# An identity product for the old state, both solve copies on ScalarE, and one matrix that adds and centers the two directions in an RWKV-7 recurrence

## The chip, the cores and the metric

One NeuronCore of a Trainium2 chip runs the whole program: a trunk of four layers (gated spatial units, an RWKV-7 mixer, latent attention, gated spatial units again) on 256 context and 256 input positions of width 1024. The metric is the device time of one execution in microseconds (us). The engines are TensorE (PE; its weight loads are shown apart as PEld), VectorE (DVE), ScalarE (ACT), GpSimd (POOL) and SyncE (SP), which issues most of the transfers. PE writes only into PSUM, an accumulation memory of eight banks; DVE and ACT read it.

## The reference, cut to what matters

The change lies in the RWKV-7 mixer, the second layer. Its recurrence runs over the positions in both directions, the context first, and carries one 64x64 state per head and direction:

```
def step(S, inp):
    w_t, k_t, v_t, kk_t, a_t = inp[:5]
    s_kk = einsum('nbhvk,nbhk->nbhv', S, kk_t)
    S = S * w_t[..., None, :] - s_kk[..., :, None] * (kk_t * a_t)[..., None, :] \
        + v_t[..., :, None] * k_t[..., None, :]
    y_t = einsum('nbhvk,nbhk->nbhv', S, inp[5])
    return S, y_t
...
y = ys[0] + jnp.flip(ys[1], axis=1)          # forward + reversed backward

yh = split_heads(y)                          # group norm over each head's 64 values
mean = jnp.mean(yh, axis=-1, keepdims=True)
var = jnp.mean(jnp.square(yh - mean), axis=-1, keepdims=True)
yn = ((yh - mean) * lax.rsqrt(var + RWKV_LN_EPS)).reshape(y.shape) * ln_gain + ln_bias
```

## The kernel before, in words

The 16 heads are taken in four groups g = 0 to 3 of four heads. The 512 positions are cut into chunks of 64, so each group has eight chunk steps (i = 0 to 7), four for the context (c = 0) and four for the input (c = 1). A step treats four "lanes" l (two directions by two pairs of heads), each with two heads h, which lie in partitions 0 to 63 and 64 to 127.

Five flows, written as generators, are interleaved in the program text in fixed ratios:

- `features` (L639 to L704) makes the per-position factors of the next group: decay scans, exponentials and the operands `AR` and `BK`, on PE, ACT, DVE and POOL.
- `inverse` (L706 to L770) inverts the triangular matrices of the next group: 31 pairs of DVE instructions, `tmp` (L734) and `Tm` (L735), each needing the one before it, and then small products on PE.
- `operands` (L774 to L807) masks products (`pe` on PE, `E` on DVE, L789) and transposes (`pbk`, `BKT`) for the next two steps.
- `chain` (L809 to L876) is the recurrence, described below.
- `gate`, `normed` and `added` (L878 to L973): products `pg` for the gate, the group norm, and the output projection `op`, which is added to `xT`.

One step of `chain`: 16 products into `pz` (the last eight read the old state `s0`), copied to `Z` by ACT; eight products into `pu`, the solve, copied into `UV` in two halves, partitions 64 to 127 by ACT (L839) and partitions 0 to 63 by DVE (L840); eight products `py` of the old state (L845); eight products `pd` (L852), to which DVE adds the old state (L856) and which it then scales by the chunk's decay (L857) to give the new state `S`; eight more products into `py` (L861). Then `Y` takes the outputs of the step. The two directions reach a place of `Y` at different steps: whichever comes first is copied there by ACT (L870, steps with c < 2), the other is added by DVE (L872, steps with c >= 2), the backward one with its positions reversed.

`normed` multiplies `Y` by `bdm`, a block matrix of 1/64, into `pmean` (L937), subtracts that from `Y` on DVE (L938), squares on ACT (L941), multiplies by `bdm` again into `pvar` (L943), takes Ln and Exp on ACT (L278, L279), and multiplies `Y` by the result on DVE (L945).

PSUM in this part: one bank each for the tags f, n and t, two for s, three for c. All of `pz`, `pu`, `py`, `pd` and `pg`, and for g < 3 `pmean`, `pvar`, `bon` and `op`, take turns in the three banks of c. The order on each engine is not the order of the text: a scheduler places the instructions when the program is built, with its own estimate of durations, and gives out the buffers as it goes; each engine then runs its own list in that order.

Of the kernel before, what the change touches and what calls it, by code (L numbers as in the profile page):

```python
# [8 lines left out]
F32 = mybir.dt.float32  # L9
F32R = mybir.dt.float32r  # L10
AF = mybir.ActivationFunctionType
ALU = mybir.AluOpType
# [86 lines left out]
def body(tc, I, out):  # L99
    nc = tc.nc  # L100
# [347 lines left out]
    def rwkv(m):  # L448
# [3 lines left out]
        bdm = const.tile([128, 128], F32, name="bdm")  # L452
        V.tensor_scalar(bdm, bd, 1.0 / 64, None, ALU.mult)
        half = const.tile([128, 5, 8], F32, name="half")
        V.tensor_scalar(half[:, 0:4, :], vec[:, 6:10, :], 0.5, None, ALU.mult)
# [353 lines left out]
        def chain(g, f):  # L809
# [4 lines left out]
            for i in range(8):  # L814
# [24 lines left out]
                S.copy(uv[H[1], 0, ii], pu[H[1]])  # L839
                V.tensor_copy(uv[H[0], 1, ii], pu[H[0]])  # L840

# [7 lines left out]
                if i < 7:  # L849
                    pd = q4(ps("pd", "c"))  # L850
                    for l, h in LH:
                        PE.matmul(pd[H[h], l], bk[:, l, h, :], uv[:, h, ii, l], start=True, stop=True)  # L852
                    sn = ct("S", [128, 4, 64], 2)
                    pcb = f["12"][:, :, i:i + 1].to_broadcast([128, 4, 64])
                    if s0 is not None:
                        V.tensor_tensor(sn, pd, s0, ALU.add)  # L856
                        V.tensor_tensor(sn, sn, pcb, ALU.mult)  # L857
                    else:
                        V.tensor_tensor(sn, pd, pcb, ALU.mult)
                for l, h in LH:  # L860
# [5 lines left out]
                c, yt = i % 4, f["Y"][i // 4]  # L866
                for n in range(2):
                    y = yt[:, :, (3 - c) * 64:(4 - c) * 64][:, :, ::-1] if n else yt[:, :, c * 64:c * 64 + 64]
                    if c < 2:
                        S.copy(y, py[:, n * 2:n * 2 + 2])  # L870
                    else:
                        V.tensor_tensor(y, y, py[:, n * 2:n * 2 + 2], ALU.add)  # L872
                if i < 7:
# [54 lines left out]
        def normed(g, f, c, b=None, q=ALL):  # L928

            if b is None:  # L930
                b = ct("fin", [128, 2, 256], 3)
                yield from bonus(g, c, b)
            cut, flat = quarters(q)
            tags = iter("fn" if g == 3 else "cc")
            y, z, b = cut(f["Y"][c]), cut(f["z"][c]), cut(b)
            pm = flat(ps("pmean", next(tags)))
            PE.matmul(pm, bdm, y, start=True, stop=True)  # L937
            V.tensor_tensor(y, y, pm, ALU.subtract)  # L938
            yield
            sq = cut(ct("fin", [128, 2, 256], 3))  # L940
            S.activation(sq, y, AF.Square)  # L941
            pq = flat(ps("pvar", next(tags)))
            PE.matmul(pq, bdm, sq, start=True, stop=True)  # L943
            state["act"] = rsqrt_bc(sq, pq, 1.0, epsln)
            V.tensor_tensor(y, y, sq, ALU.mult)  # L945
            yield
            for pr in range(2):
                o = g * 2 + pr
                V.scalar_tensor_tensor(out=y[:, pr], in0=y[:, pr], scalar=hvec[:, 1, o:o + 1], in1=b[:, pr], op0=ALU.mult, op1=ALU.add)
            state["dve"] = V.tensor_tensor(y, y, z, ALU.mult)  # L950
            yield
# [5 lines left out]
        def added(g, f, c, tags, q=ALL, ws=None):  # L957

            cut, flat = quarters(q)
            y = cut(f["Y"][c])  # L960
            for oo in range(4):
# [70 lines left out]
        for g in range(4):  # L1032
# [5 lines left out]
            for c in range(2):  # L1038
                f["Y"].append(ct("Y", [128, 2, 256], 3))
                if (g, c) == (3, 1):  # L1040
# [355 lines left out]
```

## Time and profile before

| | us |
|---|---|
| three runs: lowest, median, highest | 1627.23, 1627.66, 1628.16 |
| the profiled execution, its own time | 1626.01 |
| its span, first to last instruction | 1623.8 |
| PE busy (matmuls), weight loads | 1521.5 (94%), 1182.9 (73%) |
| DVE, ACT, POOL busy | 1173.6 (72%), 786.9 (48%), 123.3 (8%) |
| the recurrence, from the first `pz` to the last output product | about 665 to 1053 |

The span is 2.2 us shorter than the profiled execution's own time. Busy shares are of the whole span. PE's busy time is modelled from pipelined starts, so a full PE row need not be PE at its peak. Of the 388 us of the recurrence three stretches of some 41 us (699.68 to 740.52, 801.94 to 843.40 and 910.51 to 951.50) hold the DVE part of the `inverse` of groups 1, 2 and 3, and the 66 us from 972 to 1038 hold the chain of group 3, which has no next group to prepare.

### The profile page before, as it was taken

The numbers are of one execution on the slowest core, as the hardware profiler recorded it, in microseconds if no ns is written. First come the engines' busy times: TensorE is split into PE (matmuls) and PEld (weight loads), VectorE is DVE, ScalarE is ACT, GpSimd is POOL, SyncE is SP. The second block draws the span as 40 slices with busy tenths as digits, with TensorE's granted clock in tenths as the row PEclk, the third lists the DMA queues.
The fourth block names the chain that finished last, engine by engine and source line by source line (L and its number), as shares of the span: only waits on it lengthen the run. The fifth ranks groups of instructions, "written<-read, shape, count | busy, mean of one in ns | idle before, by whom it ended". The sixth has DMA issues, their size and how long they took to land.

```text
span 1623.8 us, 28689 instructions
## 1 busy us (share of the span) xinstructions
PE 1521.5 (94%) x11538; PEld 1182.9 (73%) x11538; DVE 1173.6 (72%) x2133; ACT 786.9 (48%) x1404; POOL 123.3 (8%) x156
## 2 busy tenths in 40 slices
PE   5999999999599998999999999889999999979999
PEld 2787888888466644776776777778777777768887
DVE  3789998844878376687877964778765666665876
ACT  4534321232456343435345333469876766456543
POOL 0000000000600232302203100000000000000000
PEclk9999999999799998899999999989999999989999
DMA  9675668531144552522322132144321232265552
GB/s 363 252 281 226 233 212 306 208 104 52 52 143 169 161 164 66 157 92 76 118 91 85 61 106 88 67 144 136 118 83 43 73 99 91 66 233 186 177 182 78
DMA packets 95173, 229.03 MB, mean 141 GB/s; under 512 B 26048, under 2 KB 52160, under 8 KB 80576
## 3 DMA queue, kind: packets, MB, share of 16 engines
q1 hardware_dynamic: 92736, 223.00, 40.6%
q10 hardware_dynamic: 2304, 4.20, 0.7%
q8 instruction: 91, 1.49, 0.4%
q14 instruction: 42, 0.34, 0.1%
HBM read 208.81 MB, written 17.83 MB: 140 GB/s over the span
## 4 chain that ended last, share of the span: by engine, by line
PE 49%; DVE 14%; ACT 3%; issue 2%; POOL 1%; DMA 1%; ACTq 0%; DVEq 0%
PE fm L310 5%; PE op L310 4%; PE op L966 2%; PE fm L311 2%; PE pg L895 2%; DVE Tm L735 2%; DVE tmp L734 2%; PE op L311 2%; PE pu L310 2%; PE pz L310 2%; PE po L1277 2%; PE sc L1295 2%; PE pe L785 2%; PE sc L1296 1%; DVE BK L695 1%
## 5 line engine op out<-in xcount | busy, mean ns | idle before, releaser
L184 DVE TENSOR_TENSOR lo<-raw,hi 128x2048 fp32r<-128x2048 f32 (+3 forms) x147 | 247.1, 1682 | 105.2 <-ACT hi L183 104.5
L183 ACT CAST hi<-raw 128x2048 fp32r<-128x2048 f32 (+3 forms) x161 | 212.3, 1324 | 217.5 <-PE op L314 40.5
L251 DVE SCALAR_TENSOR_TENSOR junk<-adaw,scb 128x1024 f32<-128x1024 f32 x112 | 136.8, 1222 | 8.7 <-DMA adaw<-in_ada_wT 6.7
L310 PE MATMUL op<-s,hi 128*128 128x512 f32 x256 | 91.5, 400 | 0.0
L375 PE MATMUL pv<-hi,hp 128*128 128x512 f32 x192 | 76.4, 400 | 9.1 <-ACT hi L183 6.0
L376 PE MATMUL pv<-lo,hp 128*128 128x512 f32 x192 | 76.2, 397 | 1.7 <-DVE lo L184 1.7
L310 PE MATMUL fm<-hx,hi 128*128 128x512 f32 x200 | 73.8, 409 | 4.1 <-ACT hx L304 3.8
L377 PE MATMUL pv<-hi,hp 128*128 128x512 f32 x192 | 75.9, 395 | 0.0
L311 PE MATMUL op<-s,lo 128*128 128x256 f32 x256 | 71.3, 281 | 0.0
L895 PE MATMUL pg<-xz,wz 128*128 128x256 f32 x256 | 68.7, 408 | 0.0
L313 PE MATMUL pj<-xs,hi 128*128 128x512 f32 x128 | 53.6, 420 | 12.5 <-ACT xs L304 10.2
L311 PE MATMUL fm<-hx,lo 128*128 128x256 f32 x200 | 56.6, 288 | 2.0 <-DVE lo L184 2.0
L995 PE MATMUL pv<-wv,xv 128*128 128x512 f32 x128 | 57.3, 596 | 0.0
L310 PEld LDWEIGHTS op<-s,hi 128*128 128x128 f32 x256 | 48.0, 188 | 12.4 <-issue 1.3
L314 PE MATMUL pj<-xs,hi 128*128 128x512 f32 x128 | 52.2, 408 | 5.0 <-DVE xs L305 5.0
L694 POOL TENSOR_TENSOR BK<-f 64x256 f32<-64x256 f32 x64 | 53.5, 836 | 38.1 <-DVE f L688 30.7
L785 PE MATMUL pe<-AR,BK 64*128 64x128 f32 x512 | 53.8, 306 | 2.2 <-DVE E L789 2.0
L310 PE MATMUL fm<-cq,hi 128*128 128x512 f32 x144 | 55.7, 423 | 0.0
L895 PEld LDWEIGHTS pg<-xz,wz 128*128 128x128 f32 x256 | 47.8, 198 | 10.0 <-issue 2.1
L315 PE MATMUL pj<-xs,lo 128*128 128x512 f32 x128 | 52.1, 408 | 2.2 <-DVE lo L184 2.1
L313 PE MATMUL pu<-hp,hi 128*128 128x512 f32 x128 | 50.7, 396 | 0.0
L789 DVE TENSOR_TENSOR E<-pe,masks 128x512 f32<-128x512 f32 x64 | 41.9, 683 | 12.1 <-PE pe L785 7.2
(392 smaller groups left out, 4063.2 us busy)
## 6 DMA issues: line engine op xcount, KB each, us to landing
adaw<-in_ada_wT SPq DMA_DIRECT2D x36, 1024.0 KB, 6.2
raw<-in_sgu_v SPq DMA_DIRECT2D x16, 1024.0 KB, 5.5
raw<-in_sgu_u SPq DMA_DIRECT2D x16, 1024.0 KB, 4.9
raw<-in_sgu_z SPq DMA_DIRECT2D x16, 1024.0 KB, 4.8
raw<-in_sgu_o SPq DMA_DIRECT2D x16, 1024.0 KB, 4.8
adaw<-in_ada_w SPq DMA_DIRECT2D x24, 512.0 KB, 10.0
xz<-xz SPq DMA_DIRECT2D x32, 256.0 KB, 3.0
raw<-in_ml_z SPq DMA_DIRECT2D x16, 512.0 KB, 3.7
```

The lines of the kernel that those rows point to most:

```text
L183: S.copy(hi[:, sl], raw[:, sl])
L184: (nc.gpsimd if parts > 1 and i else V).tensor_tensor(lo[:, sl], raw[:, sl], hi[:, sl], ALU.subtract)
L251: V.scalar_tensor_tensor(out=junk, in0=raw[:, f, :], scalar=1.0, in1=scb[:, c, :], op0=ALU.mult, op1=ALU.mult, accum_out=m[:, t * 2 + f, c ...
L310: PE.matmul(p, whi, x, start=start, stop=False)
L311: PE.matmul(p[:, 0:256], wlo, x[:, 0], start=False, stop=stop)
L313: PE.matmul(p, whi, x[:, 0], start=start, stop=False)
L375: PE.matmul(pv[tb], hs[k][:, 0, sl], whi[:, ws_], start=k == 0, stop=False)
L376: PE.matmul(pv[tb], hs[k][:, 0, sl], wlo[:, ws_], start=False, stop=False)
L377: PE.matmul(pv[tb], hs[k][:, 1, sl], whi[:, ws_], start=False, stop=k == 7)
L785: PE.matmul(pe[h][:, j * 128:j * 128 + 128], bk[H[h], i % 4, :, :], ar[H[h], i % 4, :, :], start=True, stop=True)
L895: PE.matmul(p, ws[k // 4][:, k % 4, pr * 128:pr * 128 + 128], xs[k // 2][:, k % 2, :], start=k == 0, stop=k == 7)
L995: PE.matmul(p, xv[:, k, tb * 128:tb * 128 + 128], ws[k // 4][:, k % 4, :], start=k == 0, stop=k == 7)
```

## The change

Three edits in the recurrence and its norm, and a buffer for them.

1. The second half of the solve copy goes from DVE to ACT (L842 of the new file), behind the first.
2. In the 24 steps that have an old state and need a new one (six in each group), two products with the identity matrix put the old state into `pd` before its own products add to it: 128 partitions by 64 columns of `ident`, once for each half of the partitions, over all 256 columns of the state. DVE then only scales.
3. Both directions' outputs are copied by ACT, the forward ones to `Y`, the backward ones (reversed) to a second tile `Yr`. The norm multiplies both by `center`, the identity minus `bdm`, into one `pmean`. That is the centered sum, so the subtraction goes, and square and scaling read `pmean`, which now keeps its bank until the scaling.

```
+        center = const.tile([128, 128], F32, name="center")
+        V.tensor_tensor(center, ident, bdm, ALU.subtract)
...
                 S.copy(uv[H[1], 0, ii], pu[H[1]])
-                V.tensor_copy(uv[H[0], 1, ii], pu[H[0]])
+                S.copy(uv[H[0], 1, ii], pu[H[0]])
...
-                    pd = q4(ps("pd", "c"))
+                    pd = ps("pd", "c")[:, 0:256]
+                    if s0 is not None:
+
+                        for h in range(2):
+                            PE.matmul(pd[H[h]], ident[:, H[h]], s0.rearrange("p l v -> p (l v)"), start=True, stop=False, skip_group_check=True)
+                    pd = pd.rearrange("p (l v) -> p l v", l=4)
                     for l, h in LH:
-                        PE.matmul(pd[H[h], l], bk[:, l, h, :], uv[:, h, ii, l], start=True, stop=True)
+                        PE.matmul(pd[H[h], l], bk[:, l, h, :], uv[:, h, ii, l], start=s0 is None and l == 0, stop=l == 3, skip_group_check=True)
                     sn = ct("S", [128, 4, 64], 2)
-                    pcb = f["12"][:, :, i:i + 1].to_broadcast([128, 4, 64])
-                    if s0 is not None:
-                        V.tensor_tensor(sn, pd, s0, ALU.add)
-                        V.tensor_tensor(sn, sn, pcb, ALU.mult)
-                    else:
-                        V.tensor_tensor(sn, pd, pcb, ALU.mult)
+                    V.tensor_tensor(sn, pd, f["12"][:, :, i:i + 1].to_broadcast([128, 4, 64]), ALU.mult)
...
-                for n in range(2):
-                    y = yt[:, :, (3 - c) * 64:(4 - c) * 64][:, :, ::-1] if n else yt[:, :, c * 64:c * 64 + 64]
-                    if c < 2:
-                        S.copy(y, py[:, n * 2:n * 2 + 2])
-                    else:
-                        V.tensor_tensor(y, y, py[:, n * 2:n * 2 + 2], ALU.add)
+                S.copy(yt[0][:, :, c * 64:c * 64 + 64], py[:, 0:2])
+                S.copy(yt[1][:, :, (3 - c) * 64:(4 - c) * 64][:, :, ::-1], py[:, 2:4])
...
-            PE.matmul(pm, bdm, y, start=True, stop=True)
-            V.tensor_tensor(y, y, pm, ALU.subtract)
+            PE.matmul(pm, center, y, start=True, stop=False)
+            PE.matmul(pm, center, cut(f["Y"][c][1]), start=False, stop=True)
             yield
             sq = cut(ct("fin", [128, 2, 256], 3))
-            S.activation(sq, y, AF.Square)
+            S.activation(sq, pm, AF.Square)
             pq = flat(ps("pvar", next(tags)))
             PE.matmul(pq, bdm, sq, start=True, stop=True)
             state["act"] = rsqrt_bc(sq, pq, 1.0, epsln)
-            V.tensor_tensor(y, y, sq, ALU.mult)
+            V.tensor_tensor(y, pm, sq, ALU.mult)
...
-                f["Y"].append(ct("Y", [128, 2, 256], 3))
+                f["Y"].append([ct("Y", [128, 2, 256], 3), ct("Yr", [128, 2, 256], 3)])
...
-    nc = _bacc.Bacc("TRN2", target_bir_lowering=False, num_devices=1)
+    nc = _bacc.Bacc("TRN2", target_bir_lowering=False, num_devices=1, dynamic_dma_scratch_size=1024)
```

The scheduler places everything anew from the first step on. On PE, the step of group 0 around the first norm's `pvar` stood thus before (`wx` and `w2w`, `l2w` are operands of `features`; in brackets the engines that a row waits for):

```order
L845 MATMUL py<-AR_3905,S 64x64 x2
L845 MATMUL py<-AR_4057,S 64x64 x2
L643 MATMUL pw<-wx,w2w 128x512
L644 MATMUL pw<-wx,l2w 128x512
L852 MATMUL pd<-UV,BKT 64x64 [waits Activation_49]
L861 MATMUL py<-E,UV 64x64
L852 MATMUL pd<-UV,BKT 64x64 [waits DVE_49]
L852 MATMUL pd<-UV,BKT 64x64 x6
L861 MATMUL py<-E,UV 64x64 x7
L895 MATMUL pg<-xz,wz 128x256 [waits PE_49]
```

After the change the same step reads on PE:

```order
L645 MATMUL pw<-wx,w2w 128x512
L646 MATMUL pw<-wx,l2w 128x512
L847 MATMUL py<-AR_3849,S 64x64 [waits Activation_49]
L847 MATMUL py<-AR_3849,S 64x64
L847 MATMUL py<-AR_4001,S 64x64 x2
L847 MATMUL py<-AR_3907,S 64x64 x2
L847 MATMUL py<-AR_4059,S 64x64 x2
L863 MATMUL py<-E,UV 64x64 [waits Activation_49]
L856 MATMUL pd<-S,ident 64x256 [waits PE_49,Activation_49]
L856 MATMUL pd<-S,ident 64x256
L859 MATMUL pd<-UV,BKT 64x64 x8
L863 MATMUL py<-E,UV 64x64 x7
```

The identity products stand right before the other products of `pd` and wait for ACT; of the 24 pairs, 14 have that wait, five wait for DVE, four for PE alone and one for nothing. The old-state products of `py`, which waited for nothing from ACT, now do in this step.

On ACT, at the same place before (L278 and L279 are Ln and Exp of the norm):

```order
L833 COPY Z<-pz 128x256
L278 ACT_TABLE_LOAD
L278 ACTIVATE fin<-pvar,epsln 128x512
L839 COPY UV<-pu 64x256
L279 ACT_TABLE_LOAD
L279 ACTIVATE fin<-fin 128x512
L658 ACTIVATE f<-pw,half 128x512
```

And after:

```order
L835 COPY Z<-pz 128x256
L278 ACT_TABLE_LOAD
L278 ACTIVATE fin<-pvar,epsln 128x512
L841 COPY UV<-pu 64x256
L279 ACT_TABLE_LOAD
L279 ACTIVATE fin<-fin 128x512
L842 COPY UV<-pu 64x256
```

The second solve copy stands behind a table load and the Exp. It does so in five of the seven norms over whole tiles; in the other two it follows the first copy directly.

## Rows read from the trace of the kernel before

**Rows 1.** Windows by stretch: start:end, length, busy PE, PEld, DVE, ACT, POOL, clock, DMA.
```profile
699.68:740.52 40.84, 39.16 (x563) 30.72 (x560) 39.22 (x100) 13.61 (x28) 1.49 (x1) 1.00 0.30 92
801.94:843.40 41.46, 38.35 (x557) 30.18 (x557) 39.20 (x99) 12.83 (x27) 1.51 (x1) 1.00 0.32 104
910.51:951.50 40.99, 37.56 (x555) 29.80 (x555) 39.09 (x99) 12.26 (x26) 0.00 (x0) 1.00 0.31 93
972.00:1038.00 66.00, 64.20 (x896) 50.12 (x895) 29.26 (x67) 23.20 (x51) 0.00 (x0) 1.00 0.29 97
1038.00:1053.00 15.00, 12.39 (x88) 11.42 (x86) 14.51 (x51) 10.38 (x28) 0.00 (x0) 1.00 0.01 2
sum 388.00, PE 360.61 PEld 279.90 DVE 287.90 ACT 168.45 POOL 61.02; mean PE 40.07 PEld 31.10 DVE 31.99 ACT 18.72 POOL 6.78
```

**Rows 2.** The page's chain that ended last, whole span, shares by engine.
```profile
PE 49%; DVE 14%; ACT 3%; issue 2%; POOL 1%; DMA 1%; ACTq 0%; DVEq 0%
```

**Rows 3.** Groups by line: busy us, mean ns of one, idle before and releaser.
```profile
L840 DVE COPY UV<-pu 64x256 f32<-64x256 f32 x32 | 13.1, 410 | 22.0 <-ACT UV L839 22.0
L839 ACT COPY UV<-pu 64x256 f32<-64x256 f32 x32 | 11.7, 367 | 32.9 <-PE pu L838 29.3 <-DMA xz<-xz 3.2
L856 DVE TENSOR_TENSOR S<-pd,S 128x256 f32<-128x256 f32 x24 | 10.0, 418 | 4.9 <-PE pd L852 4.8
L872 DVE TENSOR_TENSOR Y<-Y,py 128x128 f32<-128x128 f32 x32 | 8.5, 282 | 0.0
L870 ACT COPY Y<-py 128x128 f32<-128x128 f32 x32 | 7.0, 271 | 11.0 <-PE py L861 11.0
```

**Rows 4.** Instructions of tile Y: ns least/median/most, first and last start.
```profile
L938 DVE TENSOR_TENSOR Y<-Y,pmean x9: 421/681/687, 712.5 to 1040.0; 128x512 f32<-128x512 f32 x7, 128x256 f32<-128x256 f32 x2
```

**Rows 5.** PE's order of time around a step: start, length, instruction, count of records.
```profile
668.62 0.69 PE L852 MATMUL pd<-UV,BKT 128*64 128x64 f32 x16
669.14 0.64 PE L861 MATMUL py<-E,UV 128*64 128x64 f32 x16
669.70 0.32 PE L829 MATMUL pz<-UV,E 64*64 64x64 f32 x2
```

**Rows 6.** The chain that ended last, in order of time: start, us, what.
```profile
972.03 1.92 PE pg L895 x8
975.04 1.05 PE pmean L937 x2
```

**Rows 7.** Windows of the state addition L856 on DVE, by stretch: length, busy, count.
```profile
699.68:740.52 40.84, 1.63 (x4) 1.00 0.30 92
801.94:843.40 41.46, 1.25 (x3) 1.00 0.32 104
910.51:951.50 40.99, 1.41 (x4) 1.00 0.31 93
972.00:1038.00 66.00, 2.53 (x6) 1.00 0.29 97
```

**Rows 8.** Windows of the subtraction L938 on DVE, the same.
```profile
699.68:740.52 40.84, 0.68 (x1) 1.00 0.30 92
972.00:1038.00 66.00, 1.79 (x3) 1.00 0.29 97
```

**Rows 9.** Sum of the windows of L840 over the three inverse stretches.
```profile
sum 123.29, DVE 4.49; mean DVE 1.50
```

**Rows 10.** Sum of the windows of L872 over the three inverse stretches.
```profile
sum 123.29, DVE 2.23; mean DVE 0.74
```

**Rows 11.** What PE waited for from 665 to 1053: us in total, times, longest.
```profile
PE pd L852 <- DVE UV L840: 6.8, 6, 2.2
PE pd L852 <- ACT UV L839: 1.8, 5, 0.6
```

**Rows 12.** ACT's order of time at the first norm.
```profile
717.85 0.37 ACT L839 COPY UV<-pu 64x256 f32<-64x256 f32 x1
718.24 1.28 ACT L279 ACT_TABLE_LOAD   x1
719.53 0.63 ACT L279 ACTIVATE fin<-fin 128x512 f32<-128x512 f32 x1
```

More of the change, by code (lines that the diff above doesn't have):

```diff
@@ L934, in normed @@
             tags = iter("fn" if g == 3 else "cc")
-            y, z, b = cut(f["Y"][c]), cut(f["z"][c]), cut(b)
+            y, z, b = cut(f["Y"][c][0]), cut(f["z"][c]), cut(b)
             pm = flat(ps("pmean", next(tags)))
-            PE.matmul(pm, bdm, y, start=True, stop=True)
-            V.tensor_tensor(y, y, pm, ALU.subtract)
+            PE.matmul(pm, center, y, start=True, stop=False)
+            PE.matmul(pm, center, cut(f["Y"][c][1]), start=False, stop=True)
             yield
             sq = cut(ct("fin", [128, 2, 256], 3))
-            S.activation(sq, y, AF.Square)
+            S.activation(sq, pm, AF.Square)
             pq = flat(ps("pvar", next(tags)))
@@ L959, in added @@
             cut, flat = quarters(q)
-            y = cut(f["Y"][c])
+            y = cut(f["Y"][c][0])
             for oo in range(4):
```

## Prediction

> **What bounds the kernel now.** I read the page's chain of waits first, then windows cut where the work changes character, then the waits on PE. Over the whole span the chain that ended last runs half on PE, 49%, and 14% on DVE [rows 2]. The change touches only the recurrence, 665 to 1053 us, so that is where its worth has to be read. There PE is busy 360.6 of 388 us and DVE 287.9 [rows 1]. The reader is to see two regimes in the stretches. In the three that hold the DVE part of the inverse, 123.3 us together, both engines are nearly full: DVE 117.5 us, PE 115.1 us, so PE idles 8.2 us. In the last group, 972 to 1038, PE is busy 64.2 of 66 us and DVE only 29.3. The remaining 183.7 us (the total less these and the 15 us tail) hold 169.0 us of PE. So PE is the engine that has least room everywhere, and DVE is its equal in the inverse stretches only. The change takes work from DVE and gives some to ACT and some to PE.
>
> **What is removed.** From DVE: 32 solve copies, 13.1 us; 24 state additions, 10.0 us; 32 output additions, 8.5 us [rows 3]; nine subtractions, seven at 0.681 and two at about 0.42, 5.6 us [rows 4]. Together 37.2 us of busy time. In the inverse stretches, where DVE can matter, it is 4.5 (solve copies [rows 9]) + 1.63 + 1.25 + 1.41 = 4.3 (state additions [rows 7]) + 2.2 (output additions [rows 10]) + three subtractions of 0.68 (the first is shown [rows 8]), 2.0: 13.1 us.
>
> **What ACT gains.** 32 copies of 0.367 and 32 of 0.271 us [rows 3], 20.4 us on an engine that is busy 168.5 of 388 us [rows 1]. Most of that is beside other work: `Z`, `BKT` and the features' activations wait behind it for a third of a microsecond. One place is different. The order on ACT shows that in five of the seven whole-tile norms the second solve copy now stands behind a table load and the Exp: 1.28 + 0.63 us [rows 12], 1.9 us in which the second half of `UV`, and with it `pd`, the new state and the next step, cannot come. Before, DVE made that copy. But DVE was late too: PE waited 6.8 us in six places for it and 1.8 us for the first half [rows 11]. Five times 1.9 is 9.6 us, against 8.6 us now. I take the two as equal: the wait for the solve copy changes its owner, and nothing is gained from moving it.
>
> **What PE gains.** The nine `pmean` products become eighteen. One of 512 columns took 1.05 us on the chain [rows 6], so seven more cost 7.4 us, and the two quarter ones, of 256 columns, 0.48 each by the `pg` product (four in 1.92 us [rows 6]), 1.0: 8.3 us. The identity products have no row. Two bounds: the nearest row is `pd` itself, which loads the same kind of 128x64 weights and goes to the two halves of the partitions in turn. Its 16 records are eight products of 64 columns, and the next group starts 0.52 us after it [rows 5]: 65 ns for 64 columns, 0.26 us for 256, 0.52 us for a pair. The other bound is the full product of 256 columns, 0.48 us each, 0.96 us for a pair. I take 0.52, since shape, type and alternation are those of `pd`: 24 pairs, 12.5 us (the other end 23.0). As a lower end on the path, pairs that run while PE waits for `UV` anyway cost nothing, and that wait is 8.6 us in all. The order speaks against much of that: 14 of the 24 pairs wait for ACT themselves, because `pd`'s bank is the one that `pu` has until the solve copies are done, so the pair starts after the copy and not during it. `pmean` adds to this: it keeps one of the three banks of tag c from its product until the scaling, `pvar` takes a second, and the old-state products of `py` then wait for ACT as well.
>
> The scaling that remains after `pd` and the products that follow do not change in kind. `center` is one small DVE instruction well ahead of the recurrence, and on SP a few loads trade places with their neighbours; I cost both at nothing, since PE's waits in the recurrence name them nowhere, and at under a microsecond if a load came late.
>
> **The sum, by stretch.** Inverse stretches: 11 pairs (the 4, 3 and 4 state additions in them [rows 7]), 5.7 us, and three `pmean`, 3.2 us, are 8.9 us more for PE, which had 8.2 us of idle time there. DVE's relief can shrink that idle time, the solve copies behind the table load keep it up; I let 4 of the 8.2 us stay: 115.1 + 8.9 + 4.0 = 128.0 against 123.3, **+4.7**. Last group: six pairs [rows 7], 3.1 us, and two whole and one quarter `pmean` (three subtractions in it [rows 8]), 2.6 us, are 5.7 us on an engine with 1.8 us to spare, of which I let 1 go: **+4.7**. The rest: seven pairs and two `pmean`, 5.7 us; PE is about half of the chain [rows 2], so some 2.9 us of it shows. DVE loses about 24 us outside the inverse stretches and holds a seventh of the chain, 3.4 us, and ACT's copies give a little back: **0**. The tail: a quarter product of 0.48 us in, a subtraction of 0.42 us out: **0**. Together +9.4 us. The profiled execution took 1626.0 us, so 1635.4; the median of the runs shown is 1.65 us above it, which makes **1637 us** for the median.
>
> **The rivals.** *PE has room, and DVE paces the inverse (faster).* DVE is 95% busy in those stretches and its 62 `tmp` and `Tm` instructions form one serial chain with the removed ones queued between; if PE can take the extra products in its stride, each stretch shortens by what DVE loses. That is 13.1 us at most; DVE already idles 5.8 us there, waiting for others, so about two thirds, 9 us, and the last group costs perhaps 1: 1627.7 - 8 = 1619.7. For it: PE's busy time is modelled and its weight loads fill only 279.9 of 388 us, 72% [rows 1]. Against it: four `pg` products of 256 columns in a row take 1.92 us with nothing between them [rows 6], and such products do not get shorter when DVE is free. It decides from the point where PE's idle time in the inverse stretches, 8.2 us, can be cut by more than the 8.9 us that PE gains, which is to say only if the busy time is padded.
>
> The Trainium skill has a rule that takes this side: its page "Perfetto Trace Analysis", section "Identifying the Most-Contended Engine", says that matmul busy time is no good measure of how near TensorE is to its limit and that the share of weight loads should be used. By that rule TensorE has over a quarter of its time free, DVE is the contended engine of the inverse stretches, and the sum would come out as this rival's; the spacing of the `pg` products in this trace does not bear it out.
>
> *The two cancel (no change).* The pairs hide in the 8.6 us of waits for `UV`, and DVE's relief pays for the `pmean` products: 1626 to 1630, say 1628.
>
> *The banks and the table load cost more than the products (much slower).* If each of the five table-load places delays `pd` by the full 1.9 us beyond what PE waits now, and `py` with it, that is 9.6 us on top of the forecast: 1647. Against it: the scheduler put two `pw` products of the features ahead of the wait, which cover some of it.
>
> **How the numbers follow.** The forecast has a chance of 0.52 with a range of its own from 1631 to 1645, the faster rival 0.21, the cancelling 0.15, the much slower 0.12. Identity pairs at 0.96 us add 10.6 us to the forecast, 1648, and belong to its upper edge. The range for eight times in ten runs from 1621, inside the faster rival, to 1650. A measurement of this kernel tells a change from none at about 0.2%, 3.3 us, so faster is under 1624.4 and slower over 1630.9: slower gets the forecast and the last rival, 0.62 after a little is taken off for its lower edge; no change 0.17; faster 0.21.
>
> **What would show it right or wrong.** Right: in the last group PE stays as full as now and the stretch from its first `pz` to the last `op` is 4 to 6 us longer; the three inverse stretches do not shorten though DVE's busy time falls by 4 us in each; a pair of identity products takes about 0.5 us of PE; PE's wait of `pd` for DVE turns into a wait for ACT of about the same sum, longest at the norms. Wrong: inverse stretches of 37 us or less (PE had room); a wait for ACT at `pd` of under 3 us in all (the pairs and old-state products cover it); a difference that comes from stages before 665 or after 1053, where the instructions are the same.

## The result, and the profile after

The changed kernel takes 1654.21 us (median of four runs, 1653.10 to 1657.17) against 1627.91 us of the kernel before (four runs beside it): a ratio of 1.0161, 95% interval 1.0141 to 1.0182, or 26 us slower. The prediction was 1637 us with a range up to 1650. The direction was right; the size was nearly three times the forecast, and outside the range. The profiled execution has a span of 1650.8 us (1623.8 before) and a mean granted clock of 0.966 (0.971 before).

Nearly all of it lies in the recurrence. From the first copy of `Z` to the `ssq` product that follows the recurrence it is 388.3 us before and 414.6 after, 26.3 of the span's 27.0 us more. What comes earlier starts the recurrence within half a microsecond of where it did (666.0 and 666.5 us), and from that `ssq` to the last one it is 369.2 and 368.9 us. Cut at the first `Z` of each group, in us:

| group | before | after | more |
|---|---|---|---|
| 0 | 86.0 | 95.0 | 9.0 |
| 1 | 108.7 | 115.3 | 6.6 |
| 2 | 107.5 | 113.5 | 6.0 |
| 3 (no inverse beside it) | 86.0 | 90.7 | 4.7 |

The windows of the changed kernel that answer to [rows 1] come first: the three inverse stretches with the two stretches between them, a part of the last group, and the whole recurrence (start:end, length, busy PE, PEld, DVE, ACT, POOL, granted clock, DMA share, GB/s).

```profile
702.13:741.69 39.56, 35.88 (x486) 26.94 (x482) 35.78 (x84) 13.12 (x29) 1.64 (x1) 0.96 0.24 68
741.69:813.06 71.37, 66.02 (x1046) 49.16 (x1046) 45.54 (x87) 39.30 (x82) 22.03 (x27) 0.95 0.33 98
813.06:852.71 39.65, 35.13 (x511) 26.72 (x509) 36.65 (x87) 13.75 (x31) 1.57 (x1) 1.00 0.24 75
852.71:928.06 75.35, 70.39 (x1071) 52.63 (x1068) 44.54 (x85) 38.80 (x80) 22.02 (x27) 0.93 0.26 82
928.06:968.48 40.42, 35.53 (x510) 27.31 (x508) 36.49 (x87) 13.26 (x30) 0.00 (x0) 0.96 0.23 73
990.00:1065.00 75.00, 73.86 (x986) 57.20 (x983) 24.61 (x49) 29.15 (x70) 0.00 (x0) 1.00 0.27 90
665.00:1080.00 415.00, 382.75 (x5686) 293.66 (x5684) 261.70 (x572) 186.69 (x414) 59.72 (x72) 0.96 0.28 85
```

The same two stretches between the inverses, in the kernel before:

```profile
740.52:801.94 61.42, 56.46 (x941) 41.30 (x940) 47.09 (x93) 34.37 (x67) 22.00 (x27) 0.94 0.30 91
843.40:910.51 67.11, 61.84 (x994) 45.94 (x995) 48.98 (x96) 34.99 (x68) 22.65 (x27) 0.95 0.25 78
```

The reader is to see four things. DVE is relieved by 26 us over the recurrence (287.9 to 261.7), and ACT gains 18. PE is busy 22.1 us longer (360.6 to 382.8) and its idle time *rises* from 27.4 to 32.3 us: the new time is work of PE and waits of PE. The inverse stretches, where DVE was nearly full, shorten by 3.7 us in all, and their PE work falls from 115.1 to 106.5 us; the stretches between them grow by 10.0 and 8.2 us, with 9.6 and 8.6 us more PE work. So whatever DVE's relief gave in one place came back in the next, where PE is full.

What PE waited for in the recurrence after the change (us in total, times, longest), against [rows 11]:

```profile
PE pd L856 <- ACT UV L842: 8.9, 5, 1.8
PE pe L787 <- DVE E L791: 7.3, 4, 3.3
PE py L847 <- ACT fin L278: 3.2, 5, 1.5
PE pg L756 <- DVE Dm L741: 2.3, 3, 1.0
...
PE pd L856 <- DVE xT L968: 1.4, 2, 0.7
```

The wait for the solve copy has changed its owner, from DVE (6.8) and ACT (1.8) to ACT alone (8.9). New is `py` waiting for the Ln of the group norm, 3.2 us in five places. The wait for `E`, 2.0 us before and 0.7 at most in one place, has three long pieces now. One is of 3.3 us; in its neighbourhood a wait of `pz` for `z`, 3.7 us once, is gone, and I count these two against each other. The other two, of 1.9 us each (ending at 797.59 and 912.99), have no such counterpart; e1 and e2, described below, have them too, at about 1.1 us each.

The groups that answer to [rows 3] (busy us, mean ns of one, idle before and its releaser):

```profile
L856 PE MATMUL pd<-S,ident 128*64 128x256 f32 x96 | 18.1, 427 | 10.3 <-ACT UV L842 8.9 <-DVE xT L968 1.4
...
L842 ACT COPY UV<-pu 64x256 f32<-64x256 f32 x32 | 11.7, 366 | 0.7
...
L935 PE MATMUL pmean<-Y,center 128*128 128x512 f32 (+1 forms) x18 | 9.2, 591 | 1.8 <-DVE S L861 1.7
...
L936 PE MATMUL pmean<-Yr,center 128*128 128x512 f32 (+1 forms) x18 | 8.3, 545 | 0.0
```

And one of the five places, the third norm, in PE's order of time (start, length, instruction, count of records, and in brackets the idle time before):

```profile
837.50 0.49 PE L646 MATMUL pw<-wx,l2w 64*128 64x512 f32 x1
838.64 0.68 PE L847 MATMUL py<-AR,S 64*64 64x64 f32 x16 [0.66 <-ACT fin L278]
839.25 0.33 PE L863 MATMUL py<-E,UV 128*64 128x64 f32 x2
841.37 0.65 PE L856 MATMUL pd<-S,ident 128*64 128x256 f32 x4 [1.78 <-ACT UV L842]
841.85 0.64 PE L859 MATMUL pd<-UV,BKT 128*64 128x64 f32 x16
```

The same place of the first norm on ACT, against [rows 12]:

```profile
722.98 0.37 ACT L841 COPY UV<-pu 64x256 f32<-64x256 f32 x1
723.36 1.28 ACT L279 ACT_TABLE_LOAD   x1
724.66 0.63 ACT L279 ACTIVATE fin<-fin 128x512 f32<-128x512 f32 x1
725.31 0.37 ACT L842 COPY UV<-pu 64x256 f32<-64x256 f32 x1
```

PE stands still for 1.78 us at each of the five, because the second solve copy waits behind the table load and the Exp. Only then comes the pair of identity products: it occupies PE for 0.48 us (841.37 to 841.85) and, as it stands, does not use the wait.

A last difference is the granted clock. The recurrence before has three spells at 0.50, the lower of the two levels (1.2 GHz), 17.1 us in all; after it has eight, 30.7 us. Four of the new kernel's, as windows:

```profile
727.00:730.41 3.41, 3.41 (x17) 2.75 (x12) 3.41 (x9) 0.92 (x3) 1.05 (x1) 0.50 0.39 119
781.60:785.01 3.41, 3.41 (x34) 2.21 (x30) 2.53 (x8) 1.55 (x4) 1.10 (x1) 0.50 0.88 272
...
897.70:901.11 3.41, 3.41 (x33) 2.98 (x33) 3.13 (x8) 1.71 (x4) 1.49 (x1) 0.51 0.64 212
...
955.70:959.11 3.41, 2.76 (x34) 2.26 (x35) 2.27 (x6) 1.16 (x3) 0.00 (x0) 0.50 0.21 72
```

These four begin within two microseconds of the end of a 1.78 us wait, or in it (waits that end at 725.73, 780.38, 895.73 and 956.35); the wait that ends at 841.37 is followed by none, and four spells have no such wait ahead. If PE's work takes twice as long in them, 13.6 us more at the lower level are 6.8 us of PE's 22.1. This is an estimate from one execution each, and an upper one: set against all executions (last column of the table below), the clock makes some 2 us of the 26.

### The profile page after: what moved, and what is told of

It reads as the page before. It is cut to its first block, busy times and chain, and to the rows that moved or that the text cites. A ratio compares the mean times of both kernels' runs of the same rounds, so it can differ in the third digit from the quotient of the medians.

```text
span 1650.8 us, 28869 instructions
## 1 busy us (share of the span) xinstructions
PE 1544.5 (94%) x11652; PEld 1197.0 (73%) x11652; DVE 1147.1 (69%) x2037; ACT 805.2 (49%) x1468; POOL 122.2 (7%) x156
## 5 line engine op out<-in xcount | busy, mean ns | idle before, releaser
L893 PE MATMUL pg<-xz,wz 128*128 128x256 f32 x256 | 72.1, 427 | 0.0
L893 PEld LDWEIGHTS pg<-xz,wz 128*128 128x128 f32 x256 | 51.4, 212 | 11.0 <-issue 2.5
L968 DVE SCALAR_TENSOR_TENSOR xT<-op,mod,xT 128x256 f32<-128x256 f32 (+1 forms) x72 | 29.9, 446 | 33.2 <-PE op L964 33.1
L787 PEld LDWEIGHTS pe<-AR,BK 64*128 64x128 f32 x512 | 42.8, 204 | 12.6 <-DVE E L791 9.7
```

Of the source, the lines that this page charges most:

```text
L787: PE.matmul(pe[h][:, j * 128:j * 128 + 128], bk[H[h], i % 4, :, :], ar[H[h], i % 4, :, :], start=True, stop=True)
L893: PE.matmul(p, ws[k // 4][:, k % 4, pr * 128:pr * 128 + 128], xs[k // 2][:, k % 2, :], start=k == 0, stop=k == 7)
```

## The experiments

The theory after the first comparison: PE's added products show nearly in full, DVE's relief is worth nothing, and something in the combination costs more than its parts. The rival: the parts are as cheap as forecast, and ACT's queue (the copy behind the table load) costs the rest. All ratios are against the kernel before, run on the same chip.

The last column is an estimate from the times and mean granted clocks of all executions on record. The clock differs from one execution to the next, and the time goes with it: of the 57 executions of the kernel before that ran beside these, the five at 0.965 took 1630.6 us on average and the 14 at 0.971 took 1626.4. Fitted over all kernels, each with a level of its own, the time falls by 0.86 us for each 0.001 of clock. The column gives each level against that of the kernel before, which is what remains at the same clock, sure to some 1 to 2 us each. The change itself has 24.3 there.

| run | what it is | median us | ratio | 95% | us more at the same clock |
|---|---|---|---|---|---|
| e1 | identity products alone | 1637.23 | 1.0063 | 1.0048 to 1.0078 | 7.4 |
| e2 | both solve copies on ACT alone | 1629.51 | 1.0008 | 0.9993 to 1.0022 | -1.2 |
| e3 | outputs added and centered by matrix alone | 1636.05 | 1.0053 | 1.0036 to 1.0070 | 10.8 |
| e4 | old state not added at all | 1635.83 | 1.0043 | 1.0027 to 1.0058 | 1.0 |
| e5 | zero products added, DVE additions kept | 1637.22 | 1.0068 | 1.0044 to 1.0092 | 9.8 |
| e6 | change, second copy on DVE | 1648.33 | 1.0130 | 1.0098 to 1.0162 | 20.7 |
| e7 | change, bank of `pmean` freed at once | 1646.12 | 1.0108 | 1.0070 to 1.0146 | 17.1 |
| c1 | centering matrix on the added output | 1630.87 | 1.0015 | 0.9996 to 1.0033 | 2.7 |
| e8 | change with e6 and e7 | 1642.64 | 1.0085 | 1.0056 to 1.0115 | 15.3 |
| e9 | copies and centering | 1645.22 | 1.0105 | 1.0070 to 1.0139 | 13.9 |
| c2 | products to fill PE ahead of the recurrence | 1647.30 | 1.0122 | 1.0081 to 1.0163 | 22.6 |
| e10 | centering alone, bank freed | 1633.35 | 1.0041 | 1.0029 to 1.0054 | 5.6 |
| e11 | copies and identity | 1634.81 | 1.0035 | 1.0021 to 1.0049 | 7.2 |

**The three parts alone.** e1 is the kernel before with the identity products in place of DVE's addition:

```diff
-                    pd = q4(ps("pd", "c"))
+                    pd = ps("pd", "c")[:, 0:256]
+                    if s0 is not None:
+                        for h in range(2):
+                            PE.matmul(pd[H[h]], ident[:, H[h]], s0.rearrange("p l v -> p (l v)"), start=True, stop=False, ...)
...
-                        V.tensor_tensor(sn, pd, s0, ALU.add)
```

> The kernel before with the identity products alone (edit 2). Theory A (PE's work and its waits add up and nothing hides the products): 24 pairs of 0.48 us, as measured in the changed kernel, all show: 11 to 13 us slower, about 1640. Rival B (the loss comes from waits, the solve copy behind the table load and the banks that pmean keeps): these are as before here, so the products hide in the old waits for UV: at most 4 us slower, about 1630. Rival C (DVE paces the inverse stretches): DVE loses 10 us, 2 to 5 us faster.

e2 is one line, e3 the hunks of the change on `Y`, `Yr`, `center` and the norm:

```diff
-                V.tensor_copy(uv[H[0], 1, ii], pu[H[0]])
+                S.copy(uv[H[0], 1, ii], pu[H[0]])
```

> The kernel before with both solve copies on ScalarE alone (edit 1). Theory A: no work is added to PE; five waits behind a table load and the Exp, about 1.8 us each, replace waits for DVE of 8.6 us in all: within 3 us of before. Rival B: the waits at the norms are the loss: 6 to 10 us slower. Rival C: DVE loses 13 us, 4.5 of it in the inverse stretches: 3 to 5 us faster.

```diff
-            PE.matmul(pm, bdm, y, start=True, stop=True)
-            V.tensor_tensor(y, y, pm, ALU.subtract)
+            PE.matmul(pm, center, y, start=True, stop=False)
+            PE.matmul(pm, center, cut(f["Y"][c][1]), start=False, stop=True)
```

> The kernel before with both directions copied by ScalarE and added and centered by one matrix alone (edit 3). Theory A: nine more products, 8.3 us of PE, and the wait of py for the Ln (3.2 us in the changed kernel): 8 to 12 us slower, about 1637. Rival B: the same products but the kept bank costs most: over 13 us slower. Rival C: DVE loses 14 us: 2 to 4 us faster.

Measured: e1 +10.3 us, e2 no change, e3 +8.6 us. By the trace's own prices the identity products are 24 x 0.48 = 11.5 us and the `pmean` products 8.3 us, so the sums come near the prices. For e1 that is in part luck. In its trace the pair stands before the wait for `UV`, not behind it as in the changed kernel, and that wait is 3.9 us where the kernel before has 8.6, so some 4.7 us of the pairs are hidden:

```profile
PE pd L857 <- DVE UV L840: 3.9, 6, 1.1
```

Against that, e1's executions have a lower clock (0.965 to 0.967) than most of the kernel before; at the same clock e1 costs 7.4 us. e2 has the five long waits already (PE's wait of `pd` for the copy, 8.8 us in five places, longest 1.9) and costs nothing: as forecast, the wait only changes its owner. The three add to about 20 us (0.0124 of 1628); the change took 26. The surplus of 6 us has an interval of some 5 us either way when taken so, and the pairs below had to bear it out.

**Is it PE's gain or DVE's loss of work?** e4 leaves out the addition of the old state on DVE and puts nothing in its place, so the state is a part of the computation that it changes. e5 keeps the addition and has PE do the 24 pairs with a matrix of zeros.

```diff
-                    if s0 is not None:
-                        V.tensor_tensor(sn, pd, s0, ALU.add)
-                        V.tensor_tensor(sn, sn, pcb, ALU.mult)
-                    else:
-                        V.tensor_tensor(sn, pd, pcb, ALU.mult)
+                    V.tensor_tensor(sn, pd, pcb, ALU.mult)
```

> The kernel before without the addition of the old state (the state is then pd scaled; 24 DVE instructions of 0.418 us are left out, no engine gets anything for them). Theory A: DVE's work is not what the time is made of; 1 to 3 us faster, from the wait for S alone. Rival C (DVE paces): 4.3 us of it lies in the inverse stretches and all of it on the step's path: 5 to 10 us faster.

```diff
+        zero = const.tile([128, 64], F32, name="zero")
+        nc.gpsimd.memset(zero, 0.0)
...
+                    if s0 is not None:
+                        for h in range(2):
+                            PE.matmul(pd[H[h]], zero, s0.rearrange("p l v -> p (l v)"), start=True, stop=False, ...)
```

> The kernel before, its DVE additions kept, with 24 pairs of products of a zero matrix with the old state put into pd first: the identity products' work for PE and nothing taken from any engine. Theory A (PE's work shows in full): 10 to 13 us slower, like the identity products with their relief of DVE (10.3 us). Rival E (what costs is the new placement that follows when DVE's part of a step gets shorter, as in the kernel without the addition, which did less work and took 7 us more): at most 5 us slower.

e5 costs 11.0 us (its interval: 7 to 15), e1 10.3. With DVE's 10.0 us of additions or without them, the products cost the same: PE's work shows, DVE's relief doesn't. e4 was a miss for every theory. With less work it is 7 us *slower*. One stretch of its recurrence, the recurrence, and a stretch of e5's:

```profile
887.00:904.10 17.10, 17.10 (x77) 11.65 (x75) 10.81 (x21) 5.62 (x11) 6.14 (x7) 0.50 0.30 89
665.00:1064.00 399.00, 373.80 (x5571) 290.37 (x5569) 279.81 (x645) 169.04 (x350) 59.27 (x72) 0.94 0.29 88
...
890.10:910.60 20.50, 20.50 (x99) 13.86 (x96) 14.16 (x26) 5.86 (x12) 6.42 (x7) 0.50 0.26 77
```

PE has the matmuls of the kernel before (5571 records, 5570 there) and is busy 13.2 us longer. It has 44.4 us at the lower clock where that kernel has 17.1; half of the 27.3 more is 13.7. So what e4 lost is the clock. Its other executions say the same: four at a mean clock of 0.961 took 1634.7 to 1636.2 us and the one at 0.965 took 1630.1, while the kernel before took 1634.8 at 0.962 and 1629.5 to 1631.9 at 0.965. At the same clock e4 neither gains nor loses. With nothing but DVE instructions taken away, PE ran for 17 us on end at half speed in a stretch where it was busy throughout. The profiled execution of e5, which takes nothing away, has such a stretch of 20.5 us near the same place. I can say what the low clock cost there, not why it was granted.

**Who makes the surplus?** First from the side of the change: e6 gives the second solve copy back to DVE, e7 copies `pmean` out of its bank at once, e8 does both.

```diff
-                S.copy(uv[H[0], 1, ii], pu[H[0]])
+                V.tensor_copy(uv[H[0], 1, ii], pu[H[0]])
```

> The changed kernel with the second solve copy back on DVE (edits 2 and 3 without 1). Theory D (products in full, and the five waits of 1.78 us behind the table load with the half clock that follows them are a price of their own): 8.9 us of waits and some 4 to 5 us of half clock go, 1640 to 1645. Theory A alone (products, waits only change owner): 1650 to 1655, since waits for DVE take their place. The sum of the single edits (10.3 + 8.6 us) gives 1647.

```diff
+            V.tensor_copy(y, pm)
             yield
             sq = cut(ct("fin", [128, 2, 256], 3))
-            S.activation(sq, pm, AF.Square)
+            S.activation(sq, y, AF.Square)
...
-            V.tensor_tensor(y, pm, sq, ALU.mult)
+            V.tensor_tensor(y, y, sq, ALU.mult)
```

> The changed kernel with pmean copied to Y by DVE at once, so that its bank is free before the square, as before the change (DVE gets nine copies of about the subtraction's length). Rival B (the kept bank makes py wait for the Ln and moves pd behind the copies): 8 us or more faster, under 1647. Theory D: the waits behind the table load stay, only the waits for the Ln (3.2 us) go: 1650 to 1656.

e8 has the edits of both:

```diff
-                S.copy(uv[H[0], 1, ii], pu[H[0]])
+                V.tensor_copy(uv[H[0], 1, ii], pu[H[0]])
...
+            V.tensor_copy(y, pm)
```

> The changed kernel with both mendings: the second solve copy back on DVE, and pmean copied to Y by DVE at once so that its bank is free. What is left of the change is its products for PE. Theory D: 19.8 us of products (24 pairs of 0.48 us, 8.3 us for the norm) stay and nothing else does: 17 to 21 us slower than before, 1644 to 1648. If the two mendings add up (5.4 and 8.2 us were measured for each alone): 1640.

Against the changed kernel e6 is 5 us faster by the ratios (the interval takes in zero, just), e7 8.6 us (clear of zero), e8 12 us. Neither mending, nor both, comes near the kernel before. e6, at 1648, lies between the two theories; e7 came as rival B had it; e8 is faster than theory D said: with only the products left of the change, 14 of their 19.8 us show. From e6 to e8, where the bank is freed with the second copy on DVE, the gain is 7.3 us (interval 0.2 to 14), little less than from the change to e7. The trace of e7 shows what the freed bank does. PE at the third norm:

```profile
830.85 0.51 PE L847 MATMUL py<-AR,S 64*64 64x64 f32 x11
831.29 0.50 PE L646 MATMUL pw<-wx,l2w 64*128 64x512 f32 x1
831.71 0.65 PE L856 MATMUL pd<-S,ident 128*64 128x256 f32 x4
...
834.25 0.62 PE L859 MATMUL pd<-UV,BKT 128*64 128x64 f32 x13 [1.65 <-ACT UV L842]
```

ACT's queue is the same here, table load, Exp and then the copy. But with a third bank to hand the old-state products of `py` (L847) run without waiting for the Ln, and the identity pair (L856, 831.71) runs *before* the wait, where the changed kernel has it behind. PE's waits in e7:

```profile
PE pd L859 <- ACT UV L842: 8.4, 6, 1.8
PE pe L787 <- DVE E L791: 7.5, 7, 3.3
```

The wait for the copy is as long as ever (8.4 against 8.9 us), while `py`'s 3.2 us for the Ln is gone and five pairs, 2.4 us, have moved into waits: with the 0.5 that is 6.1 of the 8.6 us. The trace is of e7's fastest execution, so its clock (20.5 us at the lower level) is not set against the median. With the copy on DVE it is alike: in e6 `py` waits for the Ln and the pair stands behind, in e8 the pair runs before the wait for `UV`. A row of e6, then one of e8:

```profile
PE py L847 <- ACT fin L278: 3.2, 5, 1.5
...
PE pd L859 <- DVE UV L842: 4.2, 6, 1.2
```

Then from the side of the kernel before, by pairs of edits. e9 is the change without the identity products, e11 the change without the centering:

```diff
-                        for h in range(2):
-                            PE.matmul(pd[H[h]], ident[:, H[h]], s0.rearrange("p l v -> p (l v)"), start=True, stop=False, ...)
...
+                        V.tensor_tensor(sn, pd, s0, ALU.add)
```

> Edits 1 and 3 without the identity products. The change took some 6 us more than its three edits alone add up to (10.3, 1.3 and 8.6 us). Theory D: the surplus comes where the copy behind the table load meets the bank that pmean keeps, both of which are here: 13 to 16 us slower, 1640 to 1643. Rival (the surplus needs the identity products, which wait for the copies): the sum of the two, 10 us slower, 1637.

```diff
-            PE.matmul(pm, center, y, start=True, stop=False)
-            PE.matmul(pm, center, cut(f["Y"][c][1]), start=False, stop=True)
+            PE.matmul(pm, bdm, y, start=True, stop=True)
+            V.tensor_tensor(y, y, pm, ALU.subtract)
```

> Edits 1 and 2 without the norm's. No bank is kept. If the surplus of some 6 us over the single edits is the meeting of the kept bank with the copy behind the table load: the sum of the two, 10 to 13 us slower. If the identity products, which wait for the copies, make a surplus of their own: 15 us or more.

e11 costs 5.7 us, less than either expectation and less than e1 alone (10.3). That difference is one of the clock: at the same clock they are 7.2 and 7.4, so the second copy on ACT adds nothing to the identity products, as it adds nothing alone. e9 costs 17 us, more than either expectation, where its two parts alone add to 10; the 7 more have an interval of as much either way, and are 4 at the same clock. The centering costs 8.6 us alone and 20.5 us (26.2 less 5.7) on top of the other two edits. That difference, 12 us with an interval of about 5 either way, is the firmest sign of a combination here; at the same clock it is 6 us (17.0 less 10.8). Two rows of e9, then one of e3:

```profile
PE pd L854 <- ACT UV L842: 8.9, 5, 1.8
PE py L847 <- ACT fin L278: 3.7, 5, 1.5
...
PE pd L854 <- DVE UV L842: 0.7, 2, 0.4
```

In e3, with the second copy on DVE, `py` waits 3.2 us for the Ln and `pd` then hardly for the copy: the one wait stands in the place of the other. In e9, with the copy behind the table load, PE has both.

**Is the kept bank dear by itself?** c1 keeps the bank as the change does, without a further product and with the outputs still added on DVE; e10 is e3 with the bank freed.

```diff
-            PE.matmul(pm, bdm, y, start=True, stop=True)
-            V.tensor_tensor(y, y, pm, ALU.subtract)
+            PE.matmul(pm, center, y, start=True, stop=True)
...
-            S.activation(sq, y, AF.Square)
+            S.activation(sq, pm, AF.Square)
```

> The kernel before with its one Y (DVE's additions kept), but centered by the matrix identity minus mean in the one product it has: nine subtractions go, PE does no more, pmean keeps its bank until the scaling. Theory A: DVE's 5.6 us are not what the time is made of: 1626 to 1630. Rival B (bank): 3 to 8 us slower. Rival C (DVE paces): 2 to 3 us faster.

```diff
+            PE.matmul(pm, center, y, start=True, stop=False)
+            PE.matmul(pm, center, cut(f["Y"][c][1]), start=False, stop=True)
+            V.tensor_copy(y, pm)
...
             S.activation(sq, y, AF.Square)
```

> Edit 3 alone, with pmean copied to Y by DVE at once so that its bank is free as before. Theory A (the nine products, 8.3 us, show in full): 7 to 10 us slower, as edit 3 alone was (8.6). Rival B (in edit 3 it is the kept bank that costs, and the products hide): 1 to 4 us slower; the two mended kernels point there, since freeing the bank gave 8.6 us with the copies on ScalarE and some 7 with one on DVE.

c1 shows no change (+2.4 us, interval -0.7 to 5.4), though `py` waits for the Ln in it, 3.0 us in four places; its one product costs what the old one did and saves the subtraction. e10 is 6.7 us slower, just under what theory A gave, and e3 8.6, not to be told apart by the ratios. So the bank alone is worth some 2 us by either pair, with intervals up to 5 (2.7 and 5.1 at the same clock), and most of e3's cost is its products. Beside the identity products it is worth 7.3 us with the second copy on DVE (e6 and e8) and 8.6 with both on ACT (the change and e7); at the same clock 5.4 and 7.2. So the copy behind the table load is no condition for the bank to be dear, and that it is dearer in company than alone is likely but not shown.

**A try to win the clock back.** PE's clock is 0.57 from 640 to 665.5 us, just ahead of the recurrence, after a wait of 5.7 us for the inverse. c2 puts unread products into that inverse, fed by 15 small DVE copies, so that PE has something to do.

```diff
+                if f is fs[0] and s % 2 and s < 30:
+                    mk = st("mk", [128, 2], 4)
+                    V.tensor_copy(mk, Tm[:, 31, 0:2])
+                    for k in range(2):
+                        PE.matmul(ps("fill", "c")[0:2], mk, xv[:, k, :], start=True, stop=True)
```

> The kernel before with 30 products of 512 columns that nobody reads, in the first group's inverse (604 to 634 us), where PE has next to nothing to do; each pair waits for a two-column copy that DVE makes every second step, 15 small instructions more on its chain. Before, the clock stands at half from 634 to 662 us, after that idle stretch. If PE's idling is what drops it: the clock of 634 to 662 stays full, and the stretch, in which PE's work is on the chain, gets 5 to 12 us shorter, against 1 to 2 us for the copies: 1617 to 1625. If the half clock there comes from something else: 1 to 3 us slower.

The same 25.5 us, in c2 and then before, and c2's recurrence:

```profile
640.00:665.50 25.50, 25.50 (x120) 8.17 (x119) 6.55 (x14) 5.43 (x8) 1.89 (x2) 1.00 0.20 42
696.00:1076.00 380.00, 356.14 (x5492) 277.84 (x5488) 276.11 (x647) 160.90 (x336) 50.06 (x61) 0.98 0.29 88
```

```profile
640.00:665.50 25.50, 24.94 (x330) 20.44 (x331) 11.81 (x21) 11.61 (x21) 6.68 (x9) 0.57 0.59 171
```

The clock stayed at 1.00, but the premise was false. PE was busy until 630 us, most of it with `pv` and `prv`, and idle only for the 5.7; the fillers stood among that work and pushed the first `Z` from 666.0 to 696.5 us. 20 us slower, although the recurrence itself, from its first `Z` to the `ssq`, is 379.5 us long where the kernel before has 388.3. No run here beat the kernel before.

## Why the prediction was right in direction and wrong in size

**The prices held.** The identity pair, for which the trace had no row, was put at 0.52 us from `pd` and took 0.48; the far bound of 0.96 is out. The `pmean` products, put at 8.3 us, cost 8.6 with the bank kept (e3) and 6.7 with it freed (e10). Priced so, the products are 19.8 us. That the single edits gave 20 is luck in part: the hidden pairs of e1 and the clock stand against each other in it, and e8, with the products alone, costs 14.

**The wait for the solve copy held.** It was to change its owner, five times 1.9 us on ACT against 8.6 us before. It is 8.9 us in the five places that the order showed, and e2, the move by itself, costs nothing.

**The last group held.** +4.7 was forecast and 4.7 came from the first `Z` of group 3 to the `ssq`, the one stretch where I let nearly every product show. There the single edits add up without a surplus: cut in the same way, e1 is 2.0 us longer there, e2 0.2 shorter and e3 3.0 longer. In this stretch the group's own norms take no bank of tag c, and no table load stands between the two solve copies.

**The step that failed is the sum by stretch.** "The rest: 0" took half of 5.7 us of products as hidden, since PE is half of the whole span's chain, and set 3.4 us for DVE's relief against the other half. The inverse stretches let 4.2 of 8.2 us of PE's idle time be filled by 8.9 us of products. Of 20.8 us of products priced, 11.4 were credited away in all, which is to say that PE's idle time was to fall by 11.4 us. It *rose* by 4.9 (27.4 to 32.3 us), while PE's busy time rose by 22.1, close to the price. So the overlap is what failed, not the cost. The credit for DVE's relief was unfounded: e1 and e5 are not to be told apart whether DVE does its additions or not, and e4, which takes the additions away and adds nothing, gains nothing. The credit for filled waits has something in it, but not in the changed kernel: e1 hides some 4.7 us of pairs and e8 shows 14 of 19.8 us, since in both the pair stands before the wait for `UV`, which is 3.9 and 4.2 us there instead of 8.6. A share of the chain of the whole span, 49% PE, was used for stretches where PE is busy 92% of the time (169.0 of 183.7 us). In the changed kernel the inverse stretches did get shorter, against my forecast of 4.7 us longer and against the sign that I gave for it, that they would not shorten. But they are not the unit in which the end is set: what PE doesn't do beside the inverse it does right after, and there the two stretches grew by 18 us.

**The term that was missing: the edits in combination, about 6 us.** I had both facts in hand, the bank that `pmean` keeps with `py` behind ACT, and the copy behind the table load, and priced neither beyond the old waits. In the changed kernel `py` and then the pair of identity products stand behind ACT, with PE idle ahead of them. Freeing the bank puts the pair before the wait, and gives 8.6 us (e7, interval 1.6 to 16) or 7.3 (e6 to e8, 0.2 to 14). The prediction's rival of the banks and the table load named this place with a chance of 0.12 and 9.6 us, but by a longer wait at `pd`; that wait stayed the same, and the cost came from what no longer ran during it. The part of the bank is shown by these two pairs of runs. That the copy behind the table load is needed for it is not: e6 and e8 have the second copy on DVE.

**The clock was in no term.** The profiled executions have 13.6 us more at the lower level in the recurrence, at most an estimated 6.8 us; by all executions together it is some 2 of the 26 us. This is not a further sum on top: part of e1's and the combination's cost is clock, as the last column of the table has it, and each version moves the spells.

**The rival that PE has room** is out. It asked that products be free where DVE is relieved; e5 gives PE 11.5 us of products and takes nothing from anyone, and the time grows by 11.0 (9.8 at the same clock). The Trainium skill's page "Perfetto Trace Analysis", section "Identifying the Most-Contended Engine", would have TensorE's nearness to its limit read from MFU (the share of the peak arithmetic that is used) and from the share of weight loads. The latter is 293.66 of 415 us here, 71%, and was 72% before. The runs do not agree for this kernel: over a quarter is free by that share, and e5's products show all the same. The rival in which the two cancel is out by the time; its hidden pairs are there in e1, and not in the changed kernel.

What stays open: why e4, e5 and partly the changed kernel are granted the lower clock; how the surplus splits between order, bank and solve copies. The change's setting of the DMA scratch is in e3, e5 to e10, c1 and c2 and not in the others; c1, which has it, bounds its cost, and it was not tried by itself. Every edit also makes the scheduler place other instructions anew, so that a single term is sure to 2 or 3 us at best. A wait on the bank alone, taken away without the DVE copy of e7, was not tried.

## What to carry to other kernels

Where one engine is busy over nine tenths of a stage, count a product added to it in full unless the order shows a wait that it will run in, and give no credit for relief of the others until a run without that work has shown one; shares of the chain over the whole span don't hold for a stage. When an edit keeps a bank longer, list what could run during a wait before and can't now: the wait itself may stay the same to a few tenths while the time grows. Run the parts singly and in pairs, since the sum of singles was 20 us here and the whole 26. And set executions of the same mean clock side by side before a few us are explained: 0.001 of it went with 0.86 us here, and e4's loss of 7 us is gone in that comparison.

## What the runs showed of the hardware that was not expected

Taking 24 DVE instructions away (e4) made the kernel 7 us slower: PE spent 44.4 us of the recurrence at the lower clock instead of 17.1, 17.1 of them in one piece, from 887.0 to 904.1 us, in which it was busy all the time. e5's profiled execution has 20.5 us in one piece near there, also with PE busy throughout. Over the 57 executions of the kernel before, the time falls from 1630.6 us on average at a mean clock of 0.965 to 1626.4 at 0.971. A pair of products of 256 columns with 128x64 weights, one for each half of the partitions, takes 0.48 us, as much as one full product of 256 columns in [rows 6] (four in 1.92 us).
